# Strassen's seven block products, one level, in the gate/up product of a trunk's second feed-forward layer

## The chip, the cores and the metric

One NeuronCore of a Trainium2 chip runs the whole program. The metric is the device time of one execution in microseconds; less is better. The engines are named as in the profile: PE (matrix products; PEld is its weight load), DVE (vector), ACT (scalar), POOL (GpSimd) and SP (the queue that issues nearly all DMAs).

## The reference

A trunk of two layers works on 128 context tokens and 512 latent tokens with rows of 1024 floats. Layer 0 mixes tokens by differential attention, layer 1 by a gated linear recurrence; each is followed by a dense SwiGLU feed-forward. Every branch is normalised, shifted and scaled by a modulation of the condition vector, and added to the trunk through a gate that is also a piece of that modulation:

```python
m = silu(cond) @ w_ada + b_ada        # split into 6: shift, scale, gate (mixer), shift, scale, gate (FFN)
def swiglu(h, w_in, w_out):           # w_in: 1024 x 5632, w_out: 2816 x 1024
    gt, up = split(h @ w_in, 2)
    return (silu(gt) * up) @ w_out
x = x + m[2] * mixer(adanorm(x, g, m[0], m[1]))
x = x + m[5] * swiglu(adanorm(x, g, m[3], m[4]), w_in, w_out)
```

## The kernel before

**Products.** Each large product is made of three products of split operands: a float operand is written as a high part `wh` (rounded by ACT, line 167) and a low part `wl` (the rest, by DVE or POOL, line 171), and `hi*hi + hi*lo + lo*hi` is summed in one PSUM bank. The activations are split the same way into `Thi` and `Tlo` (lines 483 to 495). So each 128x128 weight block costs three matmuls, and each raw weight tile `wr` (128x1024 floats, 512 KB, three buffers) is loaded by SP, split by ACT, then by DVE, and only then free for the next load. The split tiles have six buffers each.

**Feed-forward** (`out_and_ffn`, line 1274, called once per layer). It begins with the rest of the mixer's output product (`last_head`, `row_sums`, tile `psr`), closes the five token tiles one after the other, normalises them (`unit_rows`), transposes and modulates them (`to_hT`). Then, for each of the 22 column tiles f of 128 columns, `ffn_in` (line 1378) computes gate and up for 320 tokens at a time: `psgu`, 8 k-blocks x 3 matmuls of 320 columns, for gate and up and for two halves of the tokens, 96 matmuls a column tile. ACT takes silu from PSUM (line 1392), DVE multiplies (1394), ACT and DVE split the result into `gT` (1395, 1396). The column tiles go in three groups (8, 7, 7); after a group `rows_out` (line 1294) multiplies its `gT` with rows of `w_ffn_out` in two halves of 512 columns (`psr`), and DVE scales by the gate and adds to the rows of the trunk (1291, 1292). In the last group of layer 1, `after` and `close` also apply the last norm and store the output.

**Modulation beside it.** `fill` is a stream of small units that are taken one after each half of `ffn_in` and one after each tile of `rows_out`. `ada_units` makes a piece of the modulation on PE (nine steps, tile `psada`); `summed_units` sums the weighted rows on DVE (`acc`, lines 291 and 293) with a short product at the end of each half. In layer 0 `fill` holds piece 5 of layer 0 by PE and pieces 0 to 4 of layer 1 by DVE; in layer 1 it holds piece 5 of layer 1 by PE.

**Order.** Each engine runs its own queue in order. The queues are ordered by a scheduler that simulates the program; where `pe["strict"]` is set PE keeps the order of the program. In layer 1 it is set from the mixer until the second column tile's first product.

Of the kernel before, what the change touches and what calls it, by code (L numbers as in the profile page):

```python
# [35 lines left out]
FF_GROUPS = [(0, 8), (8, 15), (15, 22)]  # L36


@with_exitstack
def trunk_kernel(ctx: ExitStack, tc: tile.TileContext, I, O):  # L40
    nc = tc.nc

# [48 lines left out]
    ident_r = cp.tile([P, P], F32R, name="ident_r")  # L91
    nc.vector.tensor_copy(ident_r, ident)
    mhalf = cp.tile([P, 8], F32, name="mhalf")
    nc.gpsimd.memset(mhalf, -0.5)
    ones_r = cp.tile([1, 32], F32, name="ones_r")
    nc.vector.memset(ones_r, 1.0)
# [4 lines left out]
    nc.scalar.dma_start(out=crows[0:8], in_=I["c_ctx"].rearrange("(k p) -> k p", p=P))  # L101
    nc.scalar.dma_start(out=crows[8:16], in_=I["c"][0].rearrange("(k p) -> k p", p=P))
    warm = cp.tile([1, 1], F32, name="warm")
    nc.scalar.activation(warm, ones_r[:, 0:1], AF.Silu)
# [6 lines left out]
    nc.vector.memset(cT, 0.0)  # L111
    nc.scalar.activation(cT[:, :, 0:2], psc[:, 0:16].rearrange("p (g k) -> p k g", g=2), AF.Silu)
    pick = cp.tile([P, 2, 32], F32, name="pick")
    nc.vector.memset(pick, 0.0)
    for g in range(2):
        nc.vector.memset(pick[:, g, g : g + 1], 1.0)

    vrows = xo_tile("vrows")[:, :P]
    nc.scalar.dma_start(out=vrows[0:16], in_=I["g_norm_mix"].rearrange("l (k p) -> (l k) p", p=P))
    nc.scalar.dma_start(out=vrows[16:32], in_=I["b_ada"][0, : 2 * D].rearrange("(k p) -> k p", p=P))  # L120
# [5 lines left out]
    cosT = cp.tile([P, 4, 2, DH], F32, name="cosT")  # L126
    sinT = cp.tile([P, 4, 4, DH], F32, name="sinT")
# [5 lines left out]
    # ------------------------------------------------------------ interleaving of two streams of work  # L133
# [8 lines left out]
    # ------------------------------------------------------------ weights  # L142
# [18 lines left out]

    def load_split(src, dims, lo_eng, ordered=False, slots=None):
        r = load_raw(src, dims, slots)
# [3 lines left out]
        nc.scalar.activation(hi[:, :n], r, AF.Copy)  # L167
        parts = 3 if lo_eng is nc.gpsimd else 1
# [7 lines left out]
    # ------------------------------------------------------------ modulation  # L176
    def ada(l, m, ps=None):
# [25 lines left out]
        nc.scalar.activation(R, ps, AF.Copy)  # L203
# [191 lines left out]
    def more_vectors(rows, lamx):  # L395
# [30 lines left out]
        for l in range(2):  # L426
            nc.vector.tensor_tensor(lbe[:, l], lbv[:, :, l, :], lbm, ALU.subtract)
# [3 lines left out]
        for l in range(2):  # L431
            nc.vector.tensor_tensor(lbe[:, l], lbe[:, l], lbm, ALU.mult)
# [1146 lines left out]
```

## Time and profile before

| | us |
|---|---|
| median of 3 timed runs (1851.82 to 1854.46) | 1853.18 |
| span of the profiled execution | 1850.6 |
| PE busy | 1807.3 (98%) |
| DVE busy | 1081.6 (58%) |
| ACT busy | 678.6 (37%) |
| POOL busy | 439.3 (24%) |
| moved by DMA | 190.02 MB, mean 103 GB/s |

The span runs from the first to the last instruction of the profiled execution; the timed runs lie 2.6 us above it at their median. Busy times are shares of the span. Matmuls overlap in the engine, so the duration of one is longer than the distance from its start to the next one's start; what a matmul costs in a row of them is that distance.

### The profile page before, as it was taken

What the parts mean: (1) busy time and instruction counts of PE and PEld (TensorE: products, weight loads), DVE (VectorE), ACT (ScalarE), POOL (GpSimd) and SP (SyncE); (2) the same over time, 40 slices, a digit from 0 to 9 for tenths busy, and PEclk for the clock granted to TensorE, in tenths of its full rate; (3) what the DMA queues carried; (4) which work ended last, traced back from release to release, by engine and by line L of the source; (5) the groups of instructions that cost most, each with busy time, mean ns of one, the idle gap of its engine ahead of it and who ended that gap; (6) DMA issues with size and microseconds to landing.
All of it is one profiled execution on the core that took longest, in us unless ns stands there. A gap on an engine that the chain in (4) does not pass through costs nothing.

```text
span 1850.6 us, 34604 instructions
## 1 busy us (share of the span) xinstructions
PE 1807.3 (98%) x14064; PEld 1664.6 (90%) x14064; DVE 1081.6 (58%) x1947; ACT 678.6 (37%) x1510; POOL 439.3 (24%) x620
## 2 busy tenths in 40 slices
PE   6999999999999999999999999999999999999998
PEld 5799999778998998999899999998789989998996
DVE  4888888756258546755666666676562333234234
ACT  3567666635231222122533333333352311212221
POOL 3345444325000000000255555555240000000001
PEclk8999999999999999999999999999999999999999
DMA  9511211554364434534422222212242422213211
GB/s 315 174 44 52 72 50 49 167 170 123 96 188 144 130 103 129 168 114 126 140 81 64 64 65 64 64 55 85 84 123 83 149 80 81 69 58 96 87 46 57
DMA packets 218363, 190.02 MB, mean 103 GB/s; under 512 B 9891, under 2 KB 176213, under 8 KB 218204
## 3 DMA queue, kind: packets, MB, share of 16 engines
q1 hardware_dynamic: 217398, 187.22, 32.7%
q8 instruction: 110, 1.80, 0.4%
q10 hardware_dynamic: 806, 0.60, 0.1%
q14 instruction: 49, 0.40, 0.1%
HBM read 180.40 MB, written 7.37 MB: 101 GB/s over the span
## 4 chain that ended last, share of the span: by engine, by line
PE 85%; DVE 7%; DMA 4%; ACT 2%; issue 1%; POOL 1%; SPq 0%; POOLq 0%; ACTq 0%; DVEq 0%
PE psgu L74 31%; PE psr L74 18%; PE psqkv L74 8%; PE psf L74 8%; PE psvg L74 5%; PE pso L74 3%; PE S L74 2%; PE pa L74 2%; PE po L74 1%; DMA wr<-w_ffn_in 1%; PE psada L74 1%; PE ptp L77 1%; DVE Q L1147 1%; DMA wr<-w_ada 1%; DMA ar<-w_ada 1%
## 5 line engine op out<-in xcount | busy, mean ns | idle before, releaser
L74 PE MATMUL psgu<-Tlo,wh 128*128 128x320 f32 x1408 | 435.0, 309 | 1.8 <-DVE Tlo L495 1.8
L74 PE MATMUL psgu<-Thi,wh 128*128 128x320 f32 x1408 | 436.5, 310 | 0.0
L74 PE MATMUL psgu<-Thi,wl 128*128 128x320 f32 x1408 | 434.7, 309 | 0.0
L167 ACT ACTIVATE wh<-wr 128x1024 fp32r<-128x1024 f32 (+1 forms) x224 | 225.9, 1015 | 416.0 <-DMA wr<-w_ffn_in 143.7
L171 DVE TENSOR_TENSOR wl<-wr,wh 128x1024 fp32r<-128x1024 f32 (+2 forms) x146 | 173.5, 1191 | 229.1 <-ACT wh L167 226.3
L74 PEld LDWEIGHTS psgu<-Thi,wh 128*128 128x128 f32 x1408 | 264.2, 188 | 5.7 <-issue 5.3
L74 PEld LDWEIGHTS psgu<-Tlo,wh 128*128 128x128 f32 x1408 | 264.2, 188 | 2.9 <-DVE Tlo L495 2.3
L74 PEld LDWEIGHTS psgu<-Thi,wl 128*128 128x128 f32 x1408 | 264.2, 188 | 0.0
L171 POOL TENSOR_TENSOR wl<-wr,wh 128x341 fp32r<-128x341 f32 (+2 forms) x234 | 218.6, 964 | 183.7 <-ACT wh L167 183.1
L74 PE MATMUL psr<-wh,Thi 128*128 128x512 f32 (+1 forms) x607 | 240.8, 398 | 0.5 <-ACT Thi L503 0.5
L74 PE MATMUL psr<-wh,Tlo 128*128 128x512 f32 (+1 forms) x607 | 235.8, 390 | 0.0
L74 PE MATMUL psr<-wl,Thi 128*128 128x512 f32 (+1 forms) x607 | 234.8, 388 | 0.0
L460 POOL TENSOR_TENSOR nss<-nss 128x1 f32<-128x1 f32 x24 | 7.5, 313 | 855.8 <-ACT xr L455 839.8
L74 PEld LDWEIGHTS psr<-wh,Tlo 128*128 128x128 f32 x607 | 114.3, 188 | 25.1
L74 PEld LDWEIGHTS psr<-wh,Thi 128*128 128x128 f32 x607 | 114.5, 189 | 24.8 <-issue 2.2
L74 PEld LDWEIGHTS psr<-wl,Thi 128*128 128x128 f32 x607 | 114.4, 188 | 21.8
L74 PE MATMUL psf<-Thi,wh 128*128 128x320 f32 x384 | 123.0, 320 | 0.0
L1394 DVE TENSOR_TENSOR gu<-psgu,sil 128x320 f32<-128x320 f32 x88 | 42.8, 486 | 134.0 <-PE psgu L74 134.0
L74 PE MATMUL psf<-Tlo,wh 128*128 128x320 f32 x384 | 118.5, 309 | 0.0
L74 PE MATMUL psf<-Thi,wl 128*128 128x320 f32 x384 | 118.5, 308 | 0.0
L74 PE MATMUL psqkv<-wh,Thi 128*128 128x384 f32 x320 | 109.1, 357 | 1.2 <-ACT Thi L596 1.2
L1291 DVE TENSOR_TENSOR rtmp<-psr,gate 128x512 f32<-128x512 f32 x69 | 47.3, 688 | 102.6 <-PE psr L74 99.4
(250 smaller groups left out, 3440.0 us busy)
## 6 DMA issues: line engine op xcount, KB each, us to landing
wr<-w_ffn_in SPq DMA_DIRECT2D x176, 256.0 KB
wr<-w_ada SPq DMA_DIRECT2D x72, 512.0 KB
wr<-w_ffn_out SPq DMA_DIRECT2D x40, 512.0 KB
wr<-w_in_rec SPq DMA_DIRECT2D x64, 256.0 KB
wr<-w_qkv_attn SPq DMA_DIRECT2D x64, 192.0 KB
ar<-w_ada SPq DMA_DIRECT2D x24, 512.0 KB
gate<-gdram SPq DMA_DIRECT2D x12, 512.0 KB
wr<-w_o_attn SPq DMA_DIRECT2D x8, 512.0 KB
```

What stands on the lines that cost most here:

```text
L74: in_order(nc.tensor.matmul(*a, **k))
L77: in_order(nc.tensor.transpose(*a, **k))
L167: nc.scalar.activation(hi[:, :n], r, AF.Copy)
L171: ins = lo_eng.tensor_tensor(lo[:, cs], r[:, cs], hi[:, cs], ALU.subtract)
L460: nc.gpsimd.tensor_tensor(sq[1], sq[0], sq[1], ALU.add)
L1147: nc.vector.tensor_tensor(qview, qview, view(T, n + 1, [2, nb], [-n - 1, 2], [0, m]), ALU.mult)
L1291: nc.vector.tensor_tensor(tmp, ps, gates[0 if t == 0 else 1][:, cs], ALU.mult)
L1394: nc.vector.tensor_tensor(gu, pss[1], sil, ALU.mult)
```

## The change

Layer 0 keeps its form (`out_and_ffn_0`); layer 1 gets a function of its own (`out_and_ffn_1`). There the 1024x256 weights of a column tile (gate and up) are four blocks of 512x128, and the 640x1024 activations four blocks of 320 tokens x 512. Column tiles 0 and 1 are computed as before (`whole_in`). For tiles 2 to 21 the two halves of gate and up come from seven block products of 12 matmuls each (4 k-blocks x 3), Winograd's form of Strassen's scheme: sums of activation blocks are made once (`sums`), sums of weight blocks for each tile on POOL (`ffn_weights`), and the sums of the products are made partly by accumulating further products onto a PSUM bank after a copy of it has been taken (`sum1`, `sum2`), partly on DVE and POOL. The column tiles go in six groups of 3 or 4, with one `gT` buffer. `rows_out` adds to the trunk's rows on POOL except in the last group, where both halves of a token tile are done together. The order of the rows at the start of layer 1's feed-forward is written anew, with DVE, ACT and POOL kept in program order there (`traced["order"]`), and the first weights are loaded ahead of it. Piece 5 of layer 1's modulation moves into the stream of layer 0, summed on DVE; there two units instead of one are taken after each half of tiles 2 to 4. `nc.vector`, `nc.scalar` and `nc.gpsimd` are written `VE`, `AC` and `PO` throughout; two tables of the attention move into its own pool.

```diff
+FF_GROUPS_7 = [(0, 4), (4, 8), (8, 12), (12, 15), (15, 18), (18, 22)]
+WHOLE = 2
...
             fill = chain(
-                ada_units([(l, 5)]),
+                ada_units([(0, 5)]),
                 summed_units(
-                    [(1, m) for m in range(5)] if l == 0 else [],
+                    [(1, m) for m in range(6)],
...
-                        take(fill)
+                        take(fill, 2 if f < 5 else 1)
...
+    def out_and_ffn_1(oT, w_o, open_rows, gcol, xs):
+            def half_tile(name):
+                return fp.tile([P, 512], F32, name=name, tag="h", bufs=7)
+            def xr_tile():
+                return fp.tile([P, D], F32, name="xr", tag="row", bufs=3)
+            def part_tile(name):
+                return fp.tile([P, HTOK], F32, name=name, tag="ct", bufs=5)
...
+            def rows_out(actT, parts, nk, after, n_tiles):
+                for t in range(n_tiles):
+                    for half, chunks, gates in parts:
+                        ps = mm_tile([P, 512], "psr")
+                        products = row_products(ps, actT, chunks, range(nk), t)
+                        drain(products)
+                        add_rows(ps, t, half, gates, PO if after is None else VE)
+                    if after is not None:
+                        after(t)
...
+            def sums(t):
...
+                PO.tensor_tensor(a22, a21, a22, ALU.add)
+                VE.tensor_tensor(a21, a11, a21, ALU.subtract)
+                VE.tensor_tensor(a11, a22, a11, ALU.subtract)
+                PO.tensor_tensor(s4, a12, a11, ALU.subtract)
+                split_rows([v[:, :, c0:c1] for v in S31], Hf[:, :, HTOK + c0 : HTOK + c1])
+                split_rows([v[:, 2, :, c0:c1] for v in S], a11)
...
+            def ffn_weights(f):
+                cols = slice(f * P, (f + 1) * P)
+                r1, r2 = (load_raw(wi[:, 4 * c : 4 * c + 4, :, cols], [4, 2, P]) for c in range(2))
...
+                h1 = split(b11, VE, [4, P])
+                h2 = split(x2, VE, [4, 2, P])
+                ta, tb = (xr_tile().rearrange("p (s k c) -> p s k c", s=2, k=4) for _ in range(2))
+                PO.tensor_tensor(ta[:, 0], b12, b11, ALU.subtract)
+                PO.tensor_tensor(ta[:, 1], b22, b12, ALU.subtract)
+                PO.tensor_tensor(tb[:, 0], b22, ta[:, 0], ALU.subtract)
+                PO.tensor_tensor(tb[:, 1], b21, tb[:, 0], ALU.subtract)
+                tb, ta = (
+                    split(t.rearrange("p s k c -> p (s k) c"), VE, [8, P]) for t in (tb, ta)
+                )
...
+            def ffn_in(f, w, group, i):
+                def product(ps, n, start):
+                    (wh, wl), (ah, al) = w[n], blocks[n]
+                    for k in range(4):
+                        for j, (a, b) in enumerate(((wh, ah), (wh, al), (wl, ah))):
+                            matmul(ps, a[:, k], b[:, k], start=start and k == 0 and j == 0, ...
+                sum1 = mm_tile([P, HTOK], "psgu")
+                product(sum1, 1, True)
+                a = part_tile("p1")
+                AC.activation(a, sum1, AF.Copy)
+                ps = mm_tile([P, HTOK], "psg")
+                product(ps, 2, True)
+                VE.tensor_tensor(a, a, ps, ALU.add)
+                AC.activation(a, a, AF.Silu)
+                product(sum1, 6, False)
+                b = part_tile("u2")
+                AC.activation(b, sum1, AF.Copy)
+                sum2 = mm_tile([P, HTOK], "psu")
+                product(sum2, 5, True)
+                d = part_tile("p5")
+                AC.activation(d, sum2, AF.Copy)
+                product(sum1, 7, False)
+                c = part_tile("u3")
+                AC.activation(c, sum1, AF.Copy)
+                PO.tensor_tensor(c, c, d, ALU.add)
+                product(sum2, 3, False)
+                VE.tensor_tensor(b, b, sum2, ALU.add)
+                VE.tensor_tensor(b, b, a, ALU.mult)
+                put_gT(group, i, 0, b)
+                product(sum1, 4, False)
+                e = part_tile("sil")
+                AC.activation(e, sum1, AF.Silu)
+                VE.tensor_tensor(c, c, e, ALU.mult)
+                put_gT(group, i, 1, c)
...
+                if gi == 0:
+                    turn_rows(3)
+                    modulate(3, PO)
+                    first.append([split_raw(w, VE) for w in w1])
...
+                    gus = [whole_in(first[0], 0)]
+                    turn_rows(4)
+                    modulate(4, PO)
...
+                    sums(4)
+                    weights = ffn_weights(WHOLE)
+                    traced["order"] = False
+                    pe["strict"] = False
+                    gus.append(whole_in(first[1], 0))
...
+                for f in range(max(f0, WHOLE), f1):
+                    ffn_in(f, weights if f == WHOLE else ffn_weights(f), group, f - f0)
...
+                for halves in ((0, 1),) if last else ((0,), (1,)):
```

## Rows read from the trace of the kernel before

**Rows 1.** The page's first section: span, busy time and share, instructions of each engine.
```profile
span 1850.6 us, 34604 instructions
PE 1807.3 (98%) x14064; PEld 1664.6 (90%) x14064; DVE 1081.6 (58%) x1947; ACT 678.6 (37%) x1510; POOL 439.3 (24%) x620
```

**Rows 2.** Busy time in stretches: length, then each engine's, PE clock, DMA share, GB/s.
```profile
435.60:880.00 444.40, 442.75 (x2870) 412.90 (x2869) 253.62 (x380) 111.87 (x175) 8.30 (x9) 1.00 0.44 133
...
1330.00:1390.00 60.00, 57.35 (x333) 48.53 (x331) 37.29 (x59) 31.08 (x66) 26.57 (x34) 1.00 0.46 142
...
1548.51:1647.06 98.55, 98.55 (x673) 98.55 (x673) 30.09 (x43) 26.45 (x42) 0.00 (x0) 1.00 0.27 83
...
1842.00:1850.60 8.60, 0.00 (x0) 0.00 (x0) 3.38 (x6) 1.23 (x3) 2.78 (x5) 0.65 0.32 122
```

**Rows 3.** The chain that ended last, in layer 1: start, length, what.
```profile
1372.15 1.43 PE psada L74 x24
...
1427.16 0.57 PE psada L74 x8
...
1548.51 98.55 PE psgu L74 x672
```

**Rows 4.** Groups by form, 1548.51 to 1647.06: busy, mean ns, idle before, releaser.
```profile
L74 PE MATMUL psgu<-Thi,wl 128*128 128x320 f32 x224 | 69.2, 309 | 0.0
...
L171 DVE TENSOR_TENSOR wl<-wr,wh 128x1024 fp32r<-128x1024 f32 x14 | 17.2, 1226 | 34.3 <-ACT wh L167 33.6
L167 ACT ACTIVATE wh<-wr 128x1024 fp32r<-128x1024 f32 x14 | 14.9, 1061 | 14.6 <-PE psgu L74 12.1 <-DMA wr<-w_ffn_in 2.5
...
L1394 DVE TENSOR_TENSOR gu<-psgu,sil 128x320 f32<-128x320 f32 x13 | 6.3, 488 | 30.5 <-PE psgu L74 30.5
L1395 ACT ACTIVATE Thi<-gu 128x320 fp32r<-128x320 f32 x13 | 6.1, 472 | 25.7 <-DVE gu L1394 25.7
L1392 ACT ACTIVATE sil<-psgu 128x320 f32<-128x320 f32 x14 | 6.1, 437 | 31.4 <-PE psgu L74 31.4
...
L171 DVE TENSOR_TENSOR wl<-wr,wh 128x512 fp32r<-128x512 f32 x1 | 0.7, 681 | 0.0
L167 ACT ACTIVATE wh<-wr 128x512 fp32r<-128x512 f32 x1 | 0.6, 634 | 0.7 <-PE psgu L74 0.7
```

**Rows 5.** Timeline of ACT: a silu that had waited for its bank.
```profile
1566.20 0.44 ACT L1392 ACTIVATE sil<-psgu 128x320 f32<-128x320 f32 x1 [2.21 <-PE psgu L74]
```

**Rows 6.** Timeline, POOL's 512-column sums without and with DVE's two-operand work beside them.
```profile
1370.88 2.04 POOL L493 TENSOR_TENSOR ha<-ha,adaC 128x512 f32<-128x512 f32 x2 [0.34 <-DVE ha L492]
...
438.09 3.35 POOL L493 TENSOR_TENSOR ha<-ha,adaC 128x512 f32<-128x512 f32 x2
```

**Rows 7.** Groups of the whole span: DVE's sums for the modulation; POOL's sum of rows.
```profile
L293 DVE SCALAR_TENSOR_TENSOR acc<-wr,cT,acc 128x512 f32<-128x512 f32 x140 | 97.0, 744 | 3.8 <-DMA wr<-w_ada 3.7
...
L554 POOL TENSOR_TENSOR orow<-orow,xc 128x512 f32<-128x512 f32 x10 | 13.5, 1353 | 41.4 <-DVE orow L553 41.4
```

**Rows 8.** The chain in layer 0: the longer summed unit, and a turn of the weight buffers.
```profile
698.61 0.92 PE psada L74 x24
...
748.45 3.97 DMA wr<-w_ffn_in
...
752.53 1.07 ACT wh L167
753.62 1.24 DVE wl L171
754.88 0.37 SPq L69
```

**Rows 9.** Timeline of the end: a token tile's close, then the same beside POOL's work.
```profile
1835.91 1.41 DVE L1488 SCALAR_TENSOR_TENSOR xr<-orow,rs,gf 128x512 f32<-128x512 f32 x2 [2.03 <-POOL rs L442]
...
1840.74 2.42 POOL L1456 TENSOR_TENSOR orow<-orow,gf 128x512 f32<-128x512 f32 x2
1840.81 2.90 DVE L1488 SCALAR_TENSOR_TENSOR xr<-orow,rs,gf 128x512 f32<-128x512 f32 x2 [0.45 <-POOL rs L442]
```

More of the change, by code (lines that the diff above doesn't have):

```diff
@@ L36, with __init__, __getattr__, traced_op @@
 FF_GROUPS = [(0, 8), (8, 15), (15, 22)]
+FF_GROUPS_7 = [(0, 4), (4, 8), (8, 12), (12, 15), (15, 18), (18, 22)]
+WHOLE = 2
+class Ordered:
+    def __init__(self, tc, engine, traced):
+        self.tc, self.engine, self.traced = tc, engine, traced
+    def __getattr__(self, name):
+        op = getattr(self.engine, name)
+        def traced_op(*a, **k):
+            ins = op(*a, **k)
+            if self.traced["order"] and name != "dma_start":
+                self.tc.keep_in_program_order(ins)
+            return ins
+        return traced_op
 @with_exitstack
@@ L41, in trunk_kernel @@
     nc = tc.nc
+    traced = {"order": False}
+    VE, AC, PO = (Ordered(tc, e, traced) for e in (nc.vector, nc.scalar, nc.gpsimd))
     cp = ctx.enter_context(tc.tile_pool(name="const", bufs=1))
@@ L160, in load_raw, with split, split_raw @@
         return r[:, :n]
+    def split(src, lo_eng, dims):
+        n = int(np.prod(dims))
+        out = []
+        for name in ("wh", "wl"):
+            v = wp.tile([P, 1024], F32R, name=name, tag=name, bufs=6)[:, :n]
+            if len(dims) == 2:
+                v = v.rearrange("p (a b) -> p a b", a=dims[0])
+            else:
+                v = v.rearrange("p (a b c) -> p a b c", a=dims[0], b=dims[1])
+            out.append(v)
+        AC.activation(out[0], src, AF.Copy)
+        lo_eng.tensor_tensor(out[1], src, out[0], ALU.subtract)
+        return out
     def load_split(src, dims, lo_eng, ordered=False, slots=None):
-        r = load_raw(src, dims, slots)
+        return split_raw(load_raw(src, dims, slots), lo_eng, ordered)
+    def split_raw(r, lo_eng, ordered=False):
         n = r.shape[1]
@@ L459, in sum_of @@
         if len(sq) > 1:
-            nc.gpsimd.tensor_tensor(sq[1], sq[0], sq[1], ALU.add)
+            PO.tensor_tensor(sq[1], sq[0], sq[1], ALU.add)
         return sq[-1]
@@ L1339, in out_and_ffn @@
             parts = [sums[t][1] for t in range(2) for _ in range(H - 1)]
-            ahead = {0: 10, 2: 2, 4: 2} if len(open_rows) == NT else {open_rows[0]: len(parts)}
             for t in open_rows:
-                for _ in range(ahead.get(t, 0)):
+                while parts:
                     next(parts.pop(0))
@@ L1401, in out_and_ffn @@
                     take(fill, 3)
-                    first.append(ffn_chunks(1, nc.vector))
+                    first.append(ffn_chunks(1, VE))
                     to_hT(NT - 2)
@@ L1493, in out_and_ffn, with within @@
-                    chunks = w_chunks(I["w_ffn_out"][l], f0, f1 - f0, half, nc.vector)
-                    closing = last and half == 1 and l == 1
-                    rows_out(gT, chunks, f1 - f0, gates, half, fill, within, after, NT - 1 if closing else NT)
-                    if closing:
-                        close(gT, chunks, f1 - f0)
-            return (nxt, xr) if l == 0 else None
+                        nxt = region_tiles(reg_h)
+                        pe["strict"] = True
+                        def within(t):
+                            if t >= 2:
+                                turned_to_hT(xr.pop(t - 2), ha_tile, t - 2, 1, 0, nxt, None, VE)
```

661 lines of the change are left out of this document (445 added, 216 removed).

## The prediction

> **What bounds the kernel now.** I read the page's first section, then the busy time by stretches, then the chain, then the groups inside one stretch. The first section shows PE busy in 1807.3 of 1850.6 us [rows 1]; the reader is to see that every other engine has at least four tenths of the span free. The stretches show where PE's 43 us of idle time lie: 1.65 in layer 0's feed-forward (435.6 to 880), 2.65 in the stretch where layer 1's mixer goes over into its feed-forward (1330 to 1390), none from 1548.51 to 1647.06, and 8.6 behind the last matmul; the rest lies ahead of 435.6 and in the recurrence, which the change leaves alone [rows 2]. The chain runs through PE without a break in the second group of column tiles: 672 gate/up matmuls in 98.55 us [rows 3]. So one costs 98.55/672 = 0.1467 us, not the 309 ns that the groups give as its duration [rows 4]; the difference is overlap inside the engine, and a sum by durations would promise twice the gain. PE's own work is the bound; what is taken off PE's work is gained unless something new makes PE wait.
>
> **The change, part by part.**
>
> *Block products.* Per column tile 7 products x 12 = 84 matmuls in place of 96, for 20 tiles: 240 matmuls fewer, of the same form. 240 x 0.1467 = **35.2 us off**. The output product keeps its number of matmuls.
>
> *Piece 5 of the modulation.* On PE in layer 1 it is nine steps: three at once, 1.43 us, and six of 0.57 us [rows 3], 4.85 us, all within PE's unbroken work: **4.85 off**. In layer 0 it becomes two summed units with bias, 24 records of 0.92 us each [rows 8]: **1.9 on**. Its DVE part is 28 sums of 744 ns [rows 7] and 4 shorter ones, 23 us at most, beside PE in a stretch where DVE is busy 253.6 of 444.4 us [rows 2]. Its eight loads of 512 KB go through the three raw buffers, and there is less cover: a turn of one buffer takes 0.37 + 3.97 + 1.07 + 1.24 = 6.65 us [rows 8], and the chain went through such turns in that stretch, though PE did not stand. Tiles 2 to 4 now want six loads a tile (2 weights, 4 modulation) in 96 x 0.1467 + 4 x 0.57 = 16.4 us, 2.7 us a load, against 6.65/3 = 2.2 that the buffers give. It fits. If it were all uncovered, eight loads would cost 8 x 2.2 = 18 us; if it stays covered, nothing. I take 1, near the lower end, because PE's idle time there is 1.65 us as it is.
>
> *Evictions inside a column tile.* New: four times a tile a product may only be added to a bank when ACT has copied it, and one other product lies between, 12 x 0.1467 = 1.76 us. ACT began a silu 0.09 us after its 24th matmul's place had passed (1548.51 + 120 x 0.1467 = 1566.11; it began at 1566.20 [rows 5]) and needs 0.437 [rows 4]; with as much again for the way back to PE about 0.63, so 1.13 us of slack. What stands ahead of it on ACT is at most a weight split of 1.061 us [rows 4]: covered, narrowly. Two splits ahead would cost 1.0 us. Over 80 places: 0 if the queue puts the copies first, 80 if two splits always stand there. I take **2 on**: the splits become ready in the same moment as copies that stand earlier in the program.
>
> *Load of the helpers per tile of 84 x 0.1467 = 12.3 us.* ACT: 0.634 + 3 x 1.061 for splits, 6 x 0.437 from PSUM (or silu), 2 x 0.472: 7.4 us. DVE: 0.681 + 3 x 1.226 + 4 x 0.488 + two low parts, which I count as sums, 2 x 0.488: 7.3 us [rows 4]. POOL: four sums of 512 columns and one of 320. A pair of 512-column sums took 2.04 us with no two-operand DVE work beside it and 3.35 with it [rows 6]; in the mean of a busier stretch one took 1.353 [rows 7]. So 1.02 to 1.35 each, with five eighths of that for the last: 4.7 to 6.2 us. Every engine is under 12.3 alone. They do not run freely beside each other, though: two sums of DVE that took 1.41 us took 2.90 when POOL began a pair just ahead of them [rows 9].
>
> The Trainium skill says on this, in "SBUF — State Buffer", section "Who interferes with whom", that a DVE instruction with two SBUF inputs and a GpSimd instruction that reads SBUF share one port, and that whoever comes first has it for the whole instruction. The trace agrees: 2.90 us against 1.41. By that rule the work of a tile that needs the port is POOL's 4.7 and DVE's 7.3 - 2 x 0.488 (the two that read PSUM) = 6.3, 11.0 us of 12.3: it still fits, with a tenth to spare. It speaks against the change, and it is the first rival.
>
> *Start of layer 1's feed-forward.* PE's products are the same; the order is new. The stretch has 2.65 us of PE idle [rows 2] to win. Against that stand the sums of activations: the second half of tile 0 needs token tile 4, whose modulation queues on DVE behind two weight splits (2.5 us), the sums of tiles 2 and 3 (some 5 us) and four other operations (2.7), all while PE has two half tiles (14.1 us) to do. By my count from these prices its low part comes 1 to 2 us late. Bounds -3 and +8 (the sums in full view once); I take **1.5 on**.
>
> *Groups and end.* Six groups in place of three: 30 more scale-and-add pairs, DVE 0.69 and POOL up to 1.35 [rows 7] against at least nine matmuls of 512 columns for each (by columns 0.1467 x 512/320 = 0.235 us each, an estimate: 2.1 us), so covered; POOL adds behind DVE do not hold PE, which has six banks. The last group closes a token tile in both halves: PE 24 x 0.235 = 5.6 us, DVE 4 x 0.69 + 1.41 = 4.2 plus 2.03 of waiting for POOL [rows 9] if its queue keeps the program's order: 6.2, so up to 0.6 x 4 = 2.4 us late, with the first tile's lag 4; none if the next tile's sums fill the wait. I take **1.5 on**. The 8.6 us behind the last matmul [rows 2] keep their steps.
>
> *Sum.* -35.2 - 4.85 + 1.9 + 1 + 2 + 1.5 + 1.5 = -32.1. Span 1850.6 - 32.1 = 1818.5. The timed median lies 2.6 above the profiled span, and nothing there changes: **1821 us**.
>
> **The rivals.**
>
> *1. DVE and POOL block each other.* For: 1.35 in place of 1.02 and 2.90 in place of 1.41 [rows 6, 7, 9]; before, POOL does nothing in this stretch [rows 2]. If both pay in full, DVE's cycle is 7.3 + 6.2 = 13.5 a tile, 1.2 over PE's 12.3, so 20 x 1.2 = 24 us: 1845. Against: the output products between the groups, where the lag is made up, and that DVE is idle for 5 of a tile's 12.3 us, in which POOL's steps cost it nothing.
>
> *2. Slower: the weights of a tile come too late.* A tile's weight sums need both raw tiles, then four POOL steps in a row, then ACT, then DVE. In one line: 0.37 + 3.97 (issue, landing) + 4 x 1.35 + 1.07 + 2 x 1.24 = 13.3 us, with DVE held by POOL twice, 1.02 each, 15.3. If the buffers (three raw, three for sums, six split) let the next tile's line start only when this one's has ended, PE waits 15.3 - 12.3 = 3.0 us a tile, 60 us in all: 1881. It decides from 12.3 + 38/20 = 14.2 us. Against: the third raw buffer is free for the next tile at once, POOL's first two steps free the first raw tile, and the split buffers of the first product come free seven products before they are wanted again. So the line should run ahead, not in step.
>
> *3. The gain is not there because each copy is paid.* If PE's queue were ordered so that the products of one bank follow each other, every copy would stand in line: 80 x 0.63 = 50 us, 1869. Against: the scheduler sees the wait and has another product to put there.
>
> The Trainium skill's "Perfetto Trace Analysis", section "Matmuls", advises that independent groups rotate through PSUM banks so that the eviction of one overlaps the next; here one bank takes four products in turn. No run here shows such a bank yet; by that advice rival 3's 50 us are what is at stake.
>
> *4. Better than the forecast:* no new waits and the 2.65 us of idle won: 1853.2 - 38.2 - 3 = 1812.
>
> **How the numbers follow.** Forecast (1812 to 1830) 0.65; rival 1 (1830 to 1850) 0.17; rival 2 0.08; rival 3 0.05; better than 1812 0.05. The range 1812 to 1847 holds the forecast and nearly all of rival 1. A measurement of this kernel can tell about 0.2%, 3.7 us, from no change. Faster by more than that: 0.65 + 0.05 + most of rival 1 = 0.85; within it 0.04, the top of rival 1 and mild forms of 2; slower 0.11, from rivals 2 and 3.
>
> **What would show each step.** In the profile after, the chain in a Strassen group should hold 84 matmuls per tile at 0.147 us, 12.3 us a tile, and no piece of ACT, DVE or POOL in it. PE's idle time in those stretches gives the eviction term: about 2 us in all; 20 or more, released by DVE or POOL, is rival 1; by a weight tile (`wh`, `wl`), rival 2; by an ACT copy, rival 3. DVE's mean for the 1024-column low part should rise above 1.23 us, POOL's 512-column sum lie between 1.02 and 1.35. In layer 0, PE's idle time should stay near 2 us and `psada` of layer 1 be gone. The forecast is wrong if layer 0 loses over 5 us, if the start of layer 1's feed-forward has over 6 us of PE idle, or if the mean distance of matmuls in a Strassen tile is above 0.155 us.

## The result

The changed kernel takes 1839.24 us (median of four runs, 1836.25 to 1840.24) beside 1853.13 for the kernel before: ratio 0.9924 [0.991, 0.9938]. It is 0.8% faster, with 1 outside the interval, and inside the forecast range of 1812 to 1847; but the gain is 13.9 us where 32.1 were forecast. The profiled span is 1836.7 against 1850.6 [rows 1], so the profile shows the same 13.9. The page's first section after:

```profile
span 1836.7 us, 34708 instructions
PE 1777.3 (97%) x13791; PEld 1633.1 (89%) x13791; DVE 1216.4 (66%) x2088; ACT 742.5 (40%) x1642; POOL 671.2 (37%) x774
```

PE's busy time fell by 30.0 us. To see where the rest went, cut both executions at one point, the last matmul pair of the recurrence that waits for ACT's `jk`. Timeline of PE, before and after (start, length, what, in brackets the idle time ahead of it and what ended it):

```profile
1335.34 0.49 PE L74 MATMUL po<-v,A 128*128 128x128 f32 x2 [0.52 <-ACT jk L1219]
```
```profile
1339.57 0.49 PE L96 MATMUL po<-v,A 128*128 128x128 f32 x2 [0.52 <-ACT jk L51]
```

Up to that point, called M below, the changed kernel has lost 4.2 us, all in layer 0. From M to the end (stretch, its length, PE's busy time, granted clock, DMA share, GB/s), before and after:

```profile
1335.34:1850.60 515.26, 504.63 (x3051) 0.99 0.28 86
```
```profile
1339.57:1836.70 497.13, 471.76 (x2730) 0.98 0.29 91
```

It gains 18.1 there. PE's idle time rises from 10.63 to 25.38 us, and part of the busy time of after was spent at a lower clock: in 2-us stretches, busy time x (1 - granted clock) sums to 6.18 us after and to 0.00 before. So PE's work at the full clock fell by 504.63 - (471.76 - 6.18) = 39.1 us, where the prediction wanted 35.2 + 4.85 = 40.05. The work went as forecast; 14.75 us of new idle time, 6.18 of clock and 4.2 of layer 0 took the gain back. (This measure puts the clock a little high: at 0.50 a matmul of 320 columns costs 0.267 us from start to start, at 1406.44, 1406.70 and 1406.97, in place of 0.147, so 0.45 of the busy time is lost and not 0.50. By that the 6.18 are about 5.6 and the 39.1 about 38.5.)

**The block products run as forecast.** The chain of after in a Strassen stretch (start, length, what), the answer to [rows 3]:

```profile
1477.09 1.75 PE psgu L96 x12
1478.84 1.76 PE psg L96 x12
1480.60 1.76 PE psu L96 x12
1482.36 3.51 PE psgu L96 x24
```

Twelve matmuls take 1.76 us, 0.147 each, and nothing but PE stands in the chain. From 1435 to 1800 PE is idle for 2.05 us in all; its largest waits there are 0.30 and 0.38 for `gT` of a group and 1.03 for a low part of weights.

**The start of layer 1's feed-forward took the gain.** PE's large waits after M (timeline):

```profile
1374.53 1.49 PE L99 MATMUL ntp<-ident,xr 128*128 128x128 f32 x8 [4.16 <-ACT xr L51]
1403.87 1.44 PE L96 MATMUL psgu<-Thi,wh 128*128 128x320 f32 x4 [5.38 <-ACT Thi L51]
1429.68 0.41 PE L96 MATMUL psgu<-Thi,wh 128*128 128x320 f32 x1 [2.64 <-ACT p L51]
```

Before, the two waits of that part were 1.33 and 0.61 us:

```profile
1358.13 1.27 PE L77 MATMUL ntp<-ident,xr 128*128 128x128 f32 x8 [1.33 <-ACT xr L481]
...
1390.32 0.41 PE L74 MATMUL psgu<-Tlo,wh 128*128 128x320 f32 x1 [0.61 <-DVE Tlo L495]
```

In the change, behind each of the three waits, the granted clock stands for some microseconds at half, 0.50, which is 1.2 of 2.4 GHz; a stretch in which it changes shows a value between (windows of PE, columns as above):

```profile
1375.57:1377.57 2.00, 2.00 (x8) 0.50 0.00 0
1377.57:1379.57 2.00, 2.00 (x8) 0.68 0.02 4
...
1403.57:1405.57 2.00, 1.70 (x6) 0.50 0.00 0
1405.57:1407.57 2.00, 2.00 (x10) 0.50 0.00 0
1407.57:1409.57 2.00, 2.00 (x9) 0.50 0.00 0
1409.57:1411.57 2.00, 2.00 (x16) 1.00 0.01 4
1429.57:1431.57 2.00, 1.89 (x8) 0.62 0.34 93
```

Read the counts: a busy 2-us stretch touches 9 or 10 matmuls at 0.50 and 16 at 1.00 (those that only end or begin in it are counted). So such a wait is paid twice, once as idle time and once in the matmuls behind it.

The Trainium skill says in "TensorE: Matmul & The Clock Gate", section "What's actually happening", that half rate is the default state of this clock and that activity lifts it. The rows agree: 0.50 within a microsecond or so behind the waits, 1.00 some microseconds of work later.

What ended the 4.16 us is seen on POOL and ACT (timeline):

```profile
1362.85 5.80 POOL L51 TENSOR_TENSOR wl<-wr,wh 128x341 fp32r<-128x341 f32 x6 [2.40 <-PE ntp L99]
1368.61 2.04 POOL L51 TENSOR_TENSOR Hf<-Hf,adaC 128x512 f32<-128x512 f32 x2
...
1369.68 0.63 ACT L51 ACTIVATE A1hi<-Hf 128x512 fp32r<-128x512 f32 x1 [5.96 <-POOL Hf L51]
1371.22 0.61 ACT L51 ACTIVATE xr<-orow 128x512 f32<-128x512 f32 x1
```

POOL splits the weights of the first column tile (two raw tiles) in six pieces, 5.80 us, ahead of token tile 0's modulation. ACT stands 5.96 us for that modulation, and behind it, by the order of the program, stand the squares of token tile 2 (`xr`), for which PE waits.

The 5.38 us is DVE's queue ahead of token tile 4 (DVE, POOL, ACT in turn):

```profile
1389.32 2.56 DVE L51 TENSOR_TENSOR wl<-wr,wh 128x1024 fp32r<-128x1024 f32 x2 [2.42 <-ACT wh L51]
...
1394.12 2.56 DVE L51 TENSOR_TENSOR Tlo<-Hf,Thi 128x512 fp32r<-128x512 f32 x2 [0.24 <-ACT Thi L51]
1396.61 1.40 DVE L51 TENSOR_TENSOR Hf<-Hf 128x512 f32<-128x512 f32 x2
1398.41 2.63 DVE L51 TENSOR_TENSOR Tlo<-Hf,Thi 128x1024 fp32r<-128x1024 f32 x2 [0.40 <-ACT Thi L51]
...
1401.37 1.27 DVE L51 TENSOR_TENSOR Hf<-ntp,adaC 128x512 f32<-128x512 f32 x2
...
1402.12 2.03 POOL L51 TENSOR_TENSOR Hf<-Hf,adaC 128x512 f32<-128x512 f32 x2 [2.76 <-DVE Hf L51]
1403.19 0.63 ACT L51 ACTIVATE Thi<-Hf 128x512 fp32r<-128x512 f32 x1 [2.22 <-POOL Hf L51]
```

The 2.64 us is ACT's queue ahead of the copy `p` of the first block product, on which PE's next product in that bank waits. PE ran dry at 1427.04. ACT first stood 2.48 us for DVE's `gu` of a plain tile, and a weight split came between (timeline of ACT):

```profile
1427.88 0.47 ACT L51 ACTIVATE gT<-gu 128x320 fp32r<-128x320 f32 x1 [2.48 <-DVE gu L51]
1428.26 1.04 ACT L51 ACTIVATE wh<-xr 128x1024 fp32r<-128x1024 f32 x1
1429.20 0.42 ACT L51 ACTIVATE p<-psgu 128x320 f32<-128x320 f32 x1
```

**Layer 0.** SP's queue where the doubled modulation steps begin (start, length with its waits, what), before and after:

```profile
442.56 3.94 SPq L69 DMA_DIRECT2D wr<-w_ada  x2
447.69 14.26 SPq L69 DMA_DIRECT2D wr<-w_ffn_in  x4
```
```profile
443.19 32.56 SPq L91 DMA_DIRECT2D wr<-w_ada  x4
476.15 0.93 SPq L91 DMA_DIRECT2D wr<-w_ffn_in  x2
```

Four modulation loads now stand in a row, and the next weights of the feed-forward are not issued before 476.15. PE waits 1.10 us (at 490.47), 1.55 (502.76) and 0.22 (520.23), where it did not wait at all before; one wait of 0.47 us later in layer 0 (796.38 before) is gone. So PE idles 2.4 us more in layer 0, and with the 1.9 us of the two summed units that is the 4.2 us at M.

**The end.** The stretch behind the last matmul is 1836.7 - 1826.33 = 10.37 us; it was 8.69.

### The profile page after: what moved, and what is told of

It is laid out like the page before. It is cut to its first block, busy times and chain, and to the rows that moved or that the text cites. A ratio compares the mean times of both kernels' runs of the same rounds, so it can differ in the third digit from the quotient of the medians.

```text
span 1836.7 us, 34708 instructions
## 1 busy us (share of the span) xinstructions
PE 1777.3 (97%) x13791; PEld 1633.1 (89%) x13791; DVE 1216.4 (66%) x2088; ACT 742.5 (40%) x1642; POOL 671.2 (37%) x774
## 4 chain that ended last, share of the span: by engine, by line
PE 79%; DVE 8%; DMA 5%; ACT 3%; POOL 2%; issue 2%; SPq 0%; POOLq 0%; ACTq 0%; DVEq 0%
PE psgu L96 22%; PE psr L96 17%; PE psf L96 8%; PE psqkv L96 8%; PE psvg L96 5%; PE psu L96 4%; PE pso L96 2%; PE S L96 2%; PE psg L96 2%; PE pa L96 2%; PE po L96 1%; DVE wl L51 1%; POOL wl L51 1%; DMA wr<-w_ada 1%; DVE Q L51 1%
## 5 line engine op out<-in xcount | busy, mean ns | idle before, releaser
L51 ACT ACTIVATE wh<-wr 128x1024 fp32r<-128x1024 f32 (+2 forms) x224 | 217.2, 976 | 382.4 <-DMA wr<-w_ffn_in 110.0
L96 PE MATMUL psgu<-Thi,wh 128*128 128x320 f32 x880 | 274.0, 313 | 10.7 <-ACT Thi L51 5.4
L96 PE MATMUL psgu<-Tlo,wh 128*128 128x320 f32 x880 | 273.1, 311 | 1.2 <-DVE Tlo L51 1.2
L96 PE MATMUL psgu<-Thi,wl 128*128 128x320 f32 x880 | 272.3, 311 | 0.2 <-DVE wl L51 0.2
L96 PEld LDWEIGHTS psgu<-Thi,wh 128*128 128x128 f32 x880 | 166.5, 190 | 13.9 <-ACT Thi L51 5.6
L96 PE MATMUL psr<-wh,Thi 128*128 128x512 f32 x380 | 153.5, 406 | 0.5 <-ACT Thi L51 0.5
L96 PE MATMUL psr<-wh,Tlo 128*128 128x512 f32 x380 | 149.0, 392 | 0.0
L96 PE MATMUL psr<-wl,Thi 128*128 128x512 f32 x380 | 148.9, 392 | 0.0
L96 PE MATMUL psr<-wh,gT 128*128 128x512 f32 (+1 forms) x448 | 140.6, 388 | 1.0 <-DVE gT L51 0.7
L51 DVE SCALAR_TENSOR_TENSOR acc<-wr,cT,acc 128x512 f32<-128x512 f32 x168 | 116.3, 748 | 4.5 <-DMA wr<-w_ada 4.5
L96 PE MATMUL psqkv<-wh,Tlo 128*128 128x384 f32 x320 | 105.7, 344 | 0.6 <-DVE Tlo L51 0.6
```

The lines of the kernel that those rows point to most:

```text
L51: ins = op(*a, **k)
L96: in_order(nc.tensor.matmul(*a, **k))
```

## The experiments

All ratios are to the kernel before, run beside them on the same chip, with 95% intervals of some 0.0015 to either side. For differences of a few us I use the profiles, cut at M as above. "Clock" is the sum of busy time x (1 - granted clock); "work" is what is left when idle time and clock are taken off.

| kernel | ratio | M | M to end | PE idle | clock | work |
|---|---|---|---|---|---|---|
| before | 1 | 1335.34 | 515.26 | 10.63 | 0.00 | 504.63 |
| the change | 0.9924 | 1339.57 | 497.13 | 25.38 | 6.18 | 465.57 |
| the change again | 0.9926 | 1341.15 | 497.35 | 25.73 | 6.25 | 465.37 |
| gate_only | 1.003 | 1340.10 | 515.90 | 14.82 | 2.26 | 498.82 |
| plain_tiles | 1.0065 | 1342.56 | 523.94 | 22.33 | 4.00 | 497.61 |
| w0_dve | 0.9926 | 1340.88 | 497.62 | 27.70 | 4.33 | 465.59 |
| no_order | 0.9876 | 1340.09 | 489.31 | 19.89 | 2.85 | 466.57 |
| filler | 0.9912 | 1337.54 | 494.66 | 16.67 | 3.26 | 474.73 |
| l0_late | 0.9898 | 1339.19 | 495.91 | 24.88 | 5.27 | 465.76 |
| third_free | 0.9903 | 1338.52 | 494.48 | 22.66 | 4.67 | 467.15 |
| third_noorder | 0.9891 | 1341.13 | 490.17 | 19.93 | 2.60 | 467.64 |
| gate_back | 0.994 | 1334.23 | 505.77 | 26.85 | 7.90 | 471.02 |
| gate_back_free | 0.9876 | 1335.19 | 492.61 | 18.78 | 3.36 | 470.47 |
| late_free | 0.9873 | 1338.66 | 490.14 | 20.56 | 3.11 | 466.47 |

How far two profiles of the same code differ can be read from it: behind M, the change, its repeat and l0_late are one program (497.1, 497.4, 495.9), and so are no_order and late_free (489.3, 490.1). Ahead of M nine kernels are one program (gate_only in the old kernel's form), with M from 1337.5 to 1342.6, mean 1340.2. So differences under about 1.5 us behind M, or 3 us ahead of it in a single profile, say nothing.

**The change itself again**, beside the last three runs below (change_again). 

> The changed kernel itself, on the chip and beside the runs of the kernel before that the next three share, so that they can be compared with it and not only with the kernel before. Every theory: 0.991 to 0.9938, its interval so far.

 It gave 0.9926 [0.9909, 0.9943], with the same waits (4.14, 5.40 and 2.61 us).

**Are the block products worth what was forecast?** The changed kernel with tiles 2 to 21 as plain products (plain_tiles). (The sums that are made late overwrite the block that the second half's plain products read, so that half is computed from other data; the amount of work is that of the plain product.)

```diff
-                    ffn_in(f, weights if f == WHOLE else ffn_weights(f), group, f - f0)
+                    ch = [split_raw(r, VE) for r in whole_weights(f)]
+                    for half in range(2):
+                        put_gT(group, f - f0, half, whole_in(ch, half))
```

> The changed kernel with all 22 column tiles computed by the plain product (the sums of activations are still made, the weight sums are not): everything else, the new order at the start and the six groups among it, stays. Theory T (the tiles give what was counted, the loss lies in the start): 20 tiles x 12 x 0.1467 = 35 us slower than the change, less some 2 to 4 us for the waits ahead of the first Strassen tile and at the group ends that go with it: 1870 to 1874. Rival S (Strassen's tiles lose much of their gain to copies and to DVE and POOL): half of it, 1857 to 1861.

 It gave 1.0065 [1.005, 1.008]: 1869.1 us, 27.8 over the 1841.3 that the change's ratio gives on that chip. Its PE work is 32.0 us more. That is near the theory's 35.2 and far from the rival that block products are half lost in waits; 1869.1 lies just under the 1870 to 1874 that were stated, and the kernel before took 1855.43 on that chip. The total differs by less, since this kernel idles 3.1 us less (it has no wait of 2.64 us ahead of a first block product, though that for token tile 4 is longer, 8.80 at 1410.30) and loses 2.2 us less to the clock. Some 3 of the 35.2 us I can't place.

**What did moving piece 5 do?** The kernel before, with only that move (gate_only):

```diff
-                ada_units([(l, 5)]),
+                ada_units([(0, 5)] if l == 0 else []),
-                    [(1, m) for m in range(5)] if l == 0 else [],
+                    [(1, m) for m in range(6)] if l == 0 else [],
-                        take(fill)
+                        take(fill, 2 if l == 0 and f < 5 else 1)
```

> The kernel before with one part of the change alone: piece 5 of layer 1's modulation summed on DVE in layer 0, with two units after each half of tiles 2 to 4, and nothing of Strassen. Theory L (layer 0's stream costs what it saves): 4.9 us less in layer 1, 1.9 us more for the summed units, and the 2.9 us of new PE idle time that the trace after shows between 437.85 and 560: 0 us, within 1.5, so 1853. Rival: that idle time is made up for elsewhere and the prediction's terms hold: 3 us faster, 1850.

 Both fell: it is slower, 1.003 [1.0019, 1.004]. M comes 4.8 us later, and behind M it gains nothing, 515.90 against 515.26, though PE has 5.8 us less work there. PE's waits at the start of layer 1's feed-forward:

```profile
1362.89 1.27 PE L77 MATMUL ntp<-ident,xr 128*128 128x128 f32 x8 [1.33 <-ACT xr L481]
...
1379.18 0.63 PE L77 MATMUL ntp<-ident,xr 128*128 128x128 f32 x4 [1.17 <-DVE ha L492]
...
1383.40 0.64 PE L74 MATMUL psgu<-Tlo,wh 128*128 128x320 f32 x1 [2.50 <-DVE Tlo L495]
```

The nine steps had been cover: with them gone PE waits 4.2 us more in all, most of it for the activations, and the clock falls around the 2.50 us (2.26 us lost).

**Is it POOL's split of the first weights?** The change with those low parts on DVE (w0_dve).

```diff
-            first[0].append(split_raw(w0[0], PO))
+            first[0].append(split_raw(w0[0], VE))
```

(the second tile likewise). 

> The changed kernel with the low parts of the first column tile's weights made by DVE in place of POOL (two instructions of 128x1024 in place of six of 341). Theory O (the order written out at the start lets POOL's 5.8 us stand ahead of the modulation, and ACT, in program order, behind it): the wait of 4.2 us ahead of the third token tile's transposes goes to under 1.5, and the slow clock behind it goes with it: 4 to 6 us faster than the change, 1833 to 1835. Rival: DVE is as late as POOL was, since it closes the rows there: within 1.5 us of the change.

 The rival held: 0.9926 [0.9909, 0.9942], as the change. The wait moved and grew (PE, timeline):

```profile
1370.99 1.94 PE L99 MATMUL ntp<-ident,xr 128*128 128x128 f32 x8 [8.36 <-DVE Hf L51]
```

DVE, kept in program order, now stands 5.76 us for ACT's high part of that weight tile with the token rows behind it. So moving the split to another engine, with the order kept, wins nothing.

**Is it the order written by hand?** The change without it (no_order).

```diff
-            traced["order"] = True
```

> The changed kernel without the program order on DVE, ACT and POOL at the start of layer 1's feed-forward: the scheduler orders these three there, PE keeps its order. Theory O: the scheduler puts the splits behind the work that PE waits for, 5 to 12 us faster than the change, 1827 to 1834. Rival P (PE's own order sets the waits, whatever the others do): within 2 us of the change.

 The time held: 0.9876 [0.9861, 0.9891], and 7.8 us less behind M: 5.5 of idle time and 3.3 of clock, with 1.0 more of work. Two of the waits that are left at that place (PE, timeline; five others are 0.2 to 1.4 us):

```profile
1363.82 1.27 PE L99 MATMUL ntp<-ident,xr 128*128 128x128 f32 x8 [1.34 <-ACT xr L51]
...
1401.85 1.44 PE L96 MATMUL psgu<-Thi,wh 128*128 128x320 f32 x4 [2.77 <-ACT Thi L51]
```

The reason that was forecast, the splits ahead of token tile 2, is not where the gain lies. Up to the wait for token tile 4 PE's waits sum to 4.9 us in the change (0.25, 4.16 and 0.52) and to 4.8 here (0.32, 1.34, 0.82, 0.17, 1.41 and 0.71), and PE runs dry for token tile 4 as far behind M, 59.0 us against 58.9. Up to there the rival's account fits. The gain comes behind it: 2.77 us in place of 5.38, no wait of 2.64 for a first copy, and the clock behind these two.

**Does the low clock cost time of its own?** The change with matmuls of no use where PE waits (filler); their sums are never read.

```diff
             take(products, 2)
+            junk = mm_tile([P, 512], "psx")
+            for i in range(18):
+                matmul(junk, oT[0][:, i % 8, 0:P], w_o[1][0][0][:, 0:512], start=(i == 0), stop=(i == 17))
             turn_rows(2)
...
                     gus.append(whole_in(first[1], 0))
+                    junk = mm_tile([P, HTOK], "psx")
+                    for i in range(36):
+                        matmul(junk, first[1][0][0][:, 0:P], A1[0][:, i % 8], start=(i == 0), stop=(i == 35))
```

> The changed kernel with matmuls of no use put where PE waits at the start of layer 1's feed-forward: 18 of 512 columns ahead of the transposes of token tile 2 (18 x 0.235 = 4.2 us against a wait of 4.16) and 36 of 320 columns ahead of the second half of the first tile (36 x 0.147 = 5.3 us against 5.38). Their sums are never read. Theory: the waits end when they did, so the filling itself costs nothing, and the granted clock, which fell to 0.54 to 0.77 in the 5 us behind those waits, stays near 1.00; the 5.7 us that the low clock cost come back in good part: ratio to the kernel before 0.989 to 0.991 (the change: 0.9924). Rival, the clock of the rows is only a sign of the idle time and costs nothing of its own: 0.992 to 0.993. If the filling stands in the way of work that was ready: above 0.9935.

 The ratio, 0.9912 [0.9894, 0.993], lies between the two accounts, and its interval holds both. In the profile, behind M, 9.2 us of useless work stand in place of 8.7 us of idle time, the clock costs 2.9 us less, and the stretch is 2.5 us shorter than in the change; against the three profiles of that program (495.9 to 497.4) it is 1.3 to 2.7, so the time won is hardly above the scatter. The granted clock is plain. At the places behind M where it fell to 0.50 and 0.68 in the change (1375.57 and 1377.57 above), and where the second wait had been, it is now (windows of PE):

```profile
1373.54:1375.54 2.00, 2.00 (x12) 1.00 0.00 0
1375.54:1377.54 2.00, 2.00 (x11) 1.00 0.00 0
...
1395.00:1415.00 20.00, 20.00 (x139) 1.00 0.10 32
```

The change has 0.83 from 1395 to 1415. Part of the waiting only moved: the wait of 0.52 us at 1382.05 in the change is one of 2.12 at 1380.05 here, and one of 1.85 stands at 1423.29, with 0.50 behind each: the rest of the clock's cost. That a low clock costs time of its own is seen most directly in the change itself, in the 0.267 us from start to start in place of 0.147.

**Layer 0's doubled steps elsewhere** (l0_late).

```diff
-                        take(fill, 2 if f < 5 else 1)
+                        take(fill, 2 if 15 <= f < 18 else 1)
```

> The changed kernel, but the summed units of layer 0's modulation are taken two at a time in column tiles 15 to 17 in place of 2 to 4. Theory: the waits of 1.10, 1.55 and 0.22 us in layer 0 come from the three raw buffers, which six loads a tile fill just when the ring has no lead; with the doubling later they go, and the time falls by 2 to 3 us: ratio 0.9908 to 0.9915. Rival, the cost is of the two further units wherever they stand: the waits move to tiles 15 to 17, ratio 0.992 to 0.993.

 0.9898 [0.988, 0.9917], further than the theory's 0.9908 to 0.9915, but the interval holds that too. The three waits are gone, and SP's queue is that of before; one wait came where the doubling now is:

```profile
808.28 0.41 PE L96 MATMUL psgu<-Thi,wh 128*128 128x320 f32 x1 [1.54 <-ACT wh L51]
```

So half the theory, half the rival: of the 2.9 us of waits 1.4 are won. M of the two kernels with the late doubling lies 1.3 earlier (mean 1338.9) than that of the nine, which is within the scatter, so the time that it saves is not shown.

**Is it lack of cover ahead of token tile 4?** The change with a third plain tile, whose first half stands there, and with its weights out of the order by hand (third_free). The edit takes the weights of the first tile of block products out of that order too.

```diff
-WHOLE = 2
+WHOLE = 3
...
-                    weights = ffn_weights(WHOLE)
...
+                    first.append([split_raw(r, VE) for r in whole_weights(2)])
                     gus.append(whole_in(first[1], 0))
+                    gus.append(whole_in(first[2], 0))
```

> The changed kernel with a third column tile as a plain product: its first half is done while PE would wait for token tile 4, and its weights stand out of the order written by hand. It costs 12 matmuls more, 1.76 us. Theory: the wait of 5.38 us (released by ACT's high part of token tile 4) is a lack of cover, not of engine time; 48 matmuls, 7.0 us, fill it, the clock behind it stays near 1.00, and the time falls by 3 to 5 us net: ratio 0.990 to 0.991. Rival, DVE's queue is what ends last there: the third tile's two low parts (2.5 us) push token tile 4 back by as much, the wait stays above 3 us and the ratio is 0.992 to 0.994.

 0.9903 [0.9886, 0.992]. The forecast time holds, the forecast reason doesn't: 7 us of work were put ahead of the wait, and the wait is still there:

```profile
1409.31 1.97 PE L96 MATMUL psgu<-Thi,wh 128*128 128x320 f32 x6 [4.83 <-ACT Thi L51]
```

Counted from M, PE got token tile 4 6.5 us later than in the change (70.8 against 64.3). That is the rival's account, DVE's queue, but only 2.5 of the 6.5 us are its two low parts. POOL now makes weight sums among those of the activations, and DVE waits for POOL and takes 3.48 us for two sums that took 1.40 in the change (DVE, timeline):

```profile
1400.19 3.48 DVE L51 TENSOR_TENSOR Hf<-Hf 128x512 f32<-128x512 f32 x2 [1.87 <-POOL Hf L51]
```

The gain of 2.7 us behind M goes with the wait of 2.64 us ahead of the first tile of block products, which is gone, and its clock. Which of the edit's two parts took it away, the run can't say.

**The two together** (third_noorder). 

> The same third plain tile, and the order written by hand on DVE, ACT and POOL taken away as in the run that only took it away (0.9876). Theory, both waits (token tile 2 behind POOL's splits, token tile 4 without cover) are separate and their gains add up: 0.985 to 0.987. Rival, the free order already puts what is needed first, and the third tile only costs its 1.76 us: 0.988 to 0.989.

 The rival held: 0.9891 [0.9873, 0.9908]; behind M 490.2 against 489.3 and 490.1 without the third tile. With the free order the idle time is the same (19.9), though in other places: the wait for token tile 4 is gone, and one of 3.20 us stands ahead of the first gate/up products. The tile's 1.8 us of matmuls is of the size of the scatter.

**Piece 5 as cover in the changed kernel**, once with the order by hand (gate_back) and once without it (gate_back_free):

```diff
+                    fill = ada_units([(1, 5)])
+                    take(fill, 3)
                     turn_rows(3)
...
                     gus = [whole_in(first[0], 0)]
+                    take(fill, 3)
...
                     gus.append(whole_in(first[1], 0))
+                    take(fill, 3)
```

with `range(5)` and `take(fill)` in layer 0 as they were. 

> The changed kernel with piece 5 of layer 1's modulation on PE again, in layer 1: three steps ahead of the transposes of token tile 3 and three behind each of the first two half tiles; layer 0 has its old pace of one step a half tile. Theory, the steps were cover: layer 0 gives back its 1.9 us of PE work and its 2.9 us of waits, the 4.85 us of steps in layer 1 stand mostly where PE waits (5.38 us for token tile 4, 2.64 us ahead of the first tile of block products), and the clock behind those waits falls less: 3 to 7 us faster than the change, ratio 0.9885 to 0.991. Rival, the prediction's term (steps of PE work cost what they take, 4.85 us, against 4.8 in layer 0): the same as the change, 0.992 to 0.993. If the eight loads of 512 KB hold back those of the first tile of block products: slower than the change, above 0.994.

 It lies with the third case, on its bound: 0.994 [0.9923, 0.9957], an interval that holds the rival too. Layer 0 gave back 5.3 us (M 1334.23 against 1339.57), and layer 1 lost 8.6. The steps themselves waited for their loads, 4.14 and 3.61 us:

```profile
1381.92 1.05 PE L96 MATMUL psada<-wr,cT 128*32 128x256 f32 x8 [4.14 <-DMA wr<-w_ada]
```

Cover that has to be loaded through the three raw buffers of the weights is no cover there. 

> The same, and without the order written by hand on DVE, ACT and POOL, where PE's waits at the start of layer 1's feed-forward are 7.5 us in seven places, none above 2.8. Theory: layer 0 gives back 4.8 us, half of the 4.85 us of steps finds a wait: 2 to 3 us under the 0.9876 of the run that only took the order away, 0.986 to 0.987. Rival, the scheduler leaves no wait long enough for a step: 0.9875 to 0.989.

 0.9876 [0.9861, 0.9892]: the value is the rival's, the interval holds both. In the profile layer 0 gives back 4.9 us, and behind M the steps cost 492.6 - 489.3 = 3.3 us (2.5 against late_free) of their 4.85, so about a third to a half of them was cover, as far as two profiles that may differ by 1.5 us can say.

**The best of it:** the free order and the doubled steps late (late_free). 

> The changed kernel without the order written by hand, and with the doubled steps of layer 0's modulation in column tiles 15 to 17. Theory, the two causes are separate: 1.5 to 3 us under the run that only took the order away (0.9876), 0.986 to 0.987. Rival, what layer 0 gives back is lost again at the start of layer 1's feed-forward: 0.9875 to 0.988.

 0.9873 [0.9858, 0.9888], 1830.63 us beside 1840.03 for the change on the same chip. It lies between the two accounts, and can't be told from no_order; both beat the change and the kernel before.

## Why the prediction was wrong, and what of it was right

The gain was less than half of the forecast. The work that was to come off came off; the term that failed is the start of layer 1's feed-forward.

**Right: what bounds the kernel, and what a matmul costs.** 0.1467 us a matmul from the chain, and not the 309 ns of the group, gave 40.05 us less work; 39.1 were measured (38.5 with the clock counted by distances).

**Right: the inside of a column tile.** The evictions were put at 2 us; from 1435 to 1800 PE is idle 2.05 us in all, and none of its waits is for a copy; the one copy that PE waited for, 2.64 us, is that of the first tile. Rivals 2 and 3 did not come, but for a single wait of 1.03 us for a weight tile. Rival 1's time (1830 to 1850) holds the result, but its mechanism doesn't explain it: POOL and DVE slowed each other, more than forecast, and inside the tiles PE didn't wait for it. Groups by form in 1430 to 1600 (count, busy us, mean ns, idle ahead):

```profile
L51 DVE TENSOR_TENSOR wl<-xr,wh 128x1024 fp32r<-128x1024 f32 x18 | 29.2, 1622 | 17.5 <-ACT wh L51 17.5
L51 DVE TENSOR_TENSOR wl<-wr,wh 128x1024 fp32r<-128x1024 f32 x19 | 24.4, 1286 | 31.7 <-ACT wh L51 31.3
...
L51 POOL TENSOR_TENSOR xr<-wr,xr 128x512 f32<-128x512 f32 x16 | 24.4, 1524 | 3.1 <-DVE wl L51 2.5
L51 POOL TENSOR_TENSOR xr<-wr 128x512 f32<-128x512 f32 x16 | 22.4, 1405 | 27.6 <-DMA wr<-w_ffn_in 27.6
```

A low part that took 1226 ns [rows 4] takes 1622 where it is that of weight sums and 1286 where it is that of raw weights; a 512-column sum on POOL takes 1405 to 1524, over the 1.02 to 1.35 us of the prediction, and its sum of 320 columns 1419, so that POOL's steps of a tile come to 7.3 us where 4.7 to 6.2 were counted. The rule of the Trainium skill that the prediction cites ("SBUF — State Buffer", "Who interferes with whom") agrees with these means. Of the reasons against rival 1, DVE's idle time is there (busy 33.4 of the 60 us from 1480); that it is what saved PE was argued, and no run takes it away.

**Wrong by 15.7 us: "start of layer 1's feed-forward", +1.5 with bounds of -3 and +8.** The measured cost is 11.0 us of idle time (12.95 from M to 1430, in place of 1.94) and 6.2 of clock, 17.2. The prediction's own sign for this term, over 6 us of PE idle, came twice over. Four steps of the term failed:
- Token tile 4 was to come "1 to 2 us late". The prediction counted 10.2 us on DVE's queue from a start at once; the queue ran from 1389.32, after 2.42 us of waiting for ACT, to 1401.37, 12.05 us, before it came to that tile. The sums of tiles 2 and 3 took 7.5 us in place of 5, and POOL and ACT add their own steps behind. PE ran dry at 1398.49. Part of the 7.5 goes with rival 1's mechanism, here in a place where PE did wait: a low part of 512 columns took 0.68 us at 1391.81 with POOL idle, and the pair at 1394.12 took 1.28 each with POOL's sums beside it. No run separates that.
- No price stood for what lies ahead of the first gate/up products: 4.9 us of waits in the change, 4.16 of them behind POOL's six splits, which the order by hand puts ahead of a modulation that ACT and then PE wait for. That three engines keep the program's order was not followed to the instruction that waits at the head of each queue. Yet neither other splitting (w0_dve, 9.0 us of waits there) nor the free order (no_order, 4.8) wins this time back, so what sets it stays open.
- No price stood for the first tile of block products, whose first copy stands on ACT behind a wait for DVE and a weight split: 2.64 us.
- No term stood for the clock. Since it was 1.00 in every stretch read of before [rows 2] while PE worked, a wait was priced at its own length.

no_order shows what the order by hand costs at the first and the third of these: without it token tile 4's wait is 2.77 us, that of the first copy is gone, and with the clock behind them 7.8 of the 17.2 us come back.

**Wrong: "piece 5 of the modulation, 4.85 off".** The steps stood "all within PE's unbroken work", and so were taken as gain. gate_only shows that in the kernel before they were what kept it unbroken: 5.8 us less work, no gain. In the changed kernel the same can't be split off cleanly, as its cover needs loads; in the free order the steps cost 2.5 to 3.3 of 4.85.

**Mis-sized: the load ring of layer 0, +1 within 0 to 18.** The argument "2.7 us a load against 2.2, it fits" is a mean over three tiles; the queue issues four modulation loads in a row, and the weights stand behind them. PE waits 2.9 us there, M comes 4.2 us later (5.2 in the mean of nine kernels against three with the old pace) where 2.9 were forecast. The prediction's own sign, over 5 us lost in layer 0, is about reached; l0_late shows that the waits go with the doubled steps' place.

**Right in size, in another place: groups and end, +1.5.** The stretch behind the last matmul grew by 1.7 us, though it was to "keep its steps"; the groups cost 1.0 us of waits, within the 2.05 above. The two long steps of the end, DVE's close of token tile 3 and POOL's product for token tile 4, take about what they took (2.42 and 2.75 us against 2.90 and 2.42 [rows 9]); but they began 1.1 us ahead of the last matmul's end (1841.91) before and begin 1.7 to 1.9 us behind it (1826.33) now:

```profile
1827.98 2.42 DVE L51 SCALAR_TENSOR_TENSOR xr<-orow,rs,gf 128x512 f32<-128x512 f32 x2
...
1828.22 2.75 POOL L51 TENSOR_TENSOR orow<-orow,gf 128x512 f32<-128x512 f32 x2 [0.43 <-ACT xr L51]
```

So the sum misses by 1.0 (work) + 1.3 (layer 0) + 15.7 (start) + 0.2 (tiles, groups and end: 2.05 + 1.7 for 3.5) = 18.2, which is what 32.1 - 13.9 leaves to explain.

## What to carry to other kernels

Where one engine is the bound, price a change in two parts: the work that it takes off, which the distances in the chain give within a few per cent, and every place where that engine's queue meets work that is newly ordered; at such a place follow each engine's queue from its first waiting instruction, not only the sum of its durations. Work that is taken away from an unbroken stretch is a gain only if what follows it is ready by then: in the kernel before the nine steps that looked like cost were cover. Charge a wait of some microseconds on PE above its length, since in these runs the matmuls behind it ran at half the clock for a while. And when an edit wins the time that was forecast, look where it won it: here no_order and third_free did so in other places than the forecast named.

## What the runs showed of the hardware

At the start of layer 1's feed-forward PE's waits of 1.70 to 8.4 us were each followed by some 2 to 6 us with stretches of granted clock at 0.50 (320-column matmuls 0.267 us from start to start in place of 0.147). Single waits of 1.10 and 1.55 us in layer 0 and of 1.34 us in no_order (1363.82) left it at 1.00, while in no_order waits of 0.82, 0.17 and 1.41 us within 3.3 us were followed by 0.50. Filling two waits with matmuls of no use kept it at 1.00 behind them. One program ahead of M scattered over 5 us from kernel to kernel (1337.5 to 1342.6), more than some of the effects looked for, so that a cut at one event told more than the whole time.
